# Forgetting attention with mask and maximum in one VectorE operation, fillers at a higher rate, and memory tokens normalised when they are prepared

## Chip, cores and metric

The kernel runs on one core of one Trainium2 chip. The metric is the device time of one execution in microseconds, the median of several runs; lower is better. The engines are TensorE (PE in the profile, with its weight loads as PEld), VectorE (DVE), ScalarE (ACT), GpSimd (POOL) and SyncE (SP), whose queue issues nearly all transfers.

## The reference, cut to what matters

One layer of a hybrid decoder, all float32, 1024 tokens of width 1024, 256 memory tokens:

```python
h = rmsnorm(x, ln1);  z = h @ w_in
ml_out = mlstm(z)                     # 4 heads of width 128
s = q @ k.T * dh**-0.5 + (c_i - c_j)  # forgetting attention, 8 heads of width 64
s = where(qpos >= kpos, s, -inf)
fx_out = softmax(s) @ v
x = x + concat([ml_out, fx_out]) @ w_out
m = rmsnorm(mem, ln_mem)              # memory tokens
x = x + cross_attention(rmsnorm(x, ln_x), m, w_q, w_kv, w_o)
u = relu(rmsnorm(x, ln2) @ w_ff1);  x = x + (u * u) @ w_ff2
out = rmsnorm(x, ln_f)
```

## The kernel before, in words

**Precision and tiles.** Each float32 operand of a projection is split in a high and a low part (`split`, L128 to L136: a copy on ScalarE with rounding, then a subtraction on VectorE), and each product is three matmuls (`mm3`, L182 to L186). Tokens are taken in two halves of 512 columns. SBUF tiles come from pools with few buffers per name (`w2`, names a to y; "f" and "p" have two buffers, "y", "a" one). PSUM has eight banks: sc 3, tp 2, mm, m2 and ov one each. An instruction that wants a buffer waits until its last user is through.

**Order.** Most of the kernel is ordered by a scheduler ahead of the run: each engine gets a fixed list of instructions and works through it in order, and SP has such a list of transfers. So an instruction that waits holds everything behind it on its engine.

**Stages.** The profile's span starts with the loads of x and the first value projection. Then `mem_prepare` (L280 to L294) prepares the memory tokens: for each of four tiles of [128, 2 x 256] it loads the tile into an "f" buffer, adds its squares, multiplies by the gain of ln_mem while splitting (L135 and L136, columns of 256), and stores high and low part to `hmd` in DRAM (L292). At the end it works out the factors 1/rms of the 256 tokens, as columns (`rcol_m`) and as a row over all partitions (`row_m`). The factors are not multiplied in here; they are kept for later. `ml_project` and `ml_head` (L558 to L660, loop L673) then do the four mLSTM heads: projections with a convolution (`conv_silu`, L490 to L510), the carried state of the first half (`carried`, `carry`), and the keys and queries of forgetting attention (`fx_project`, L625 to L636), written to DRAM.

**Forgetting attention** (358 to 587 us of the span). Each of 8 heads has 8 query tiles of 128 rows. `Tile.score` (L715) makes the scores of a query tile in one or two parts of at most 512 columns: two matmuls per part and, in the last part, a third one, of the identity with a triangular constant (L724), which adds -BIG above the diagonal. `Tile.top` (L727) takes the negated maximum of each part on VectorE (L728), and for a second part the minimum of both (L731). `Tile.exp` (L733) is the exponential on ScalarE with that number as bias. `Tile.scale` divides by the sum on GpSimd. `Values` (L749 to L780) transposes the weights (L760), splits them, and multiplies them by the values (L779).

`slot` (L973) issues one step of each of these, in an order written out by hand (`in_order` fixes it on each engine). 13 lead slots issue scores alone; then come 96 value slots (8 heads, 4 + 8 key tiles each), then some that only close.

**Fillers.** Between these steps run independent matmuls, cut into steps with a cost in units: `key_unit` and `value_unit` make the keys and values of cross attention from `hmd` (8 steps of 1.5 for each of 8 + 8 groups), `out_unit` makes the first 5 of 8 slices of the output projection (5 steps of 3.0 for each of 16 groups): 432 units in all. In value slot n, steps are issued until `max(n - DELAY, 0) * RATE` units are spent (L1044: RATE 3.6, DELAY 3), at most to the end of one group. What is left after the slots is issued behind them, in one go (L1053 to L1058). The sink of a key group multiplies by `row_m` (L874) and splits and stores one slot later; that of a value group has `rcol_m` as the scale of its split.

**After it.** `out_proj` (from 607 us) adds the remaining three slices: `mix_load` (L836 to L840) reads what the last heads stored (L794, L795), and `full_sink` loads the partial sum (L1070), adds and stores. Cross attention and the MLP follow; the change doesn't touch them.

Of the kernel before, what the change touches and what calls it, by code (L numbers as in the profile page):

```python
# [9 lines left out]
F32 = mybir.dt.float32  # L10
F32R = mybir.dt.float32r
AF = mybir.ActivationFunctionType
ALU = mybir.AluOpType
# [4 lines left out]
P = 128  # L18
T = 1024
TH = 512  # L20
D = 1024
KT = D // P
NM = 256
# [8 lines left out]
BIG = 1e30  # L32
# [12 lines left out]
def hybrid_layer(ctx: ExitStack, tc: tile.TileContext, a: dict, out: bass.AP):  # L45
    nc = tc.nc
    v, s, g = nc.vector, nc.scalar, nc.gpsimd
# [31 lines left out]
    def w2(tag, n=512, dt=F32, p=P):  # L79
        return sb("r_" + tag, [P, 512], BUFS[tag], dt)[:p, :n]  # L80

    def col(tag, n=1, bufs=3):
        return sb("c_" + tag, [P, 8], bufs)[:, :n]
# [24 lines left out]
    def const(n, shape, dt=F32):  # L108
        return pool.tile(shape, dt, tag=n, name=n, bufs=1)

    load = nc.sync.dma_start
# [4 lines left out]
    ident = const("ident", [P, P])  # L116
    g.memset(ident, 1.0)
    g.affine_select(out=ident, in_=ident, pattern=[[-1, P]], compare_op=ALU.is_equal, fill=0.0, base=0, channel_multiplier=1)
    BF16 = mybir.dt.bfloat16
    identb = const("identb", [P, P], BF16)  # L120
    v.tensor_copy(identb, ident)
    causal = const("causal", [P, P], BF16)
    g.memset(causal, 0.0)
    g.affine_select(out=causal, in_=causal, pattern=[[-1, P]], compare_op=ALU.is_ge, fill=-BIG, base=0, channel_multiplier=1)
    half = const("half", [P, 8])
    g.memset(half, -0.5)
    vec = const("vec", [P, a["vec"].shape[1]])
# [1 line left out]
    def split(hi, lo, src, scale=None):  # L129

        if scale is None:
            s.activation(hi, src, AF.Copy)  # L132
            return v.tensor_tensor(out=lo, in0=src, in1=hi.bitcast(F32), op=ALU.subtract)  # L133
        else:
            s.activation(hi, src, AF.Copy, scale=scale)  # L135
            return v.scalar_tensor_tensor(out=lo, in0=src, scalar=scale, in1=hi.bitcast(F32), op0=ALU.mult, op1=ALU.subtract)  # L136
# [24 lines left out]
    def rotate(*tags):  # L161

        spare[tags] = spare.get(tags, -1) + 1
        return w2(tags[spare[tags] % len(tags)])
# [52 lines left out]
    def square_sum(acc, x, first, by=s, add=v):  # L217
        sq = acc if first else w2("c")[:, : x.shape[-1]]
        if by is s:
            s.activation(sq, x, AF.Square)  # L220
        else:
            by.tensor_tensor(out=sq, in0=x, in1=x, op=ALU.mult)
        if not first:
            add.tensor_tensor(out=acc, in0=sq, in1=acc, op=ALU.add)

    def rsqrt_sums(acc, r, nt, parts=1, bank=None, over=None):

        ps = (bank or ov_)()
        for t in range(nt):
            for e in range(parts):  # L230
                at = (e * nt + t) * P
                nc.tensor.matmul(ps[:, t : t + 1], acc[:, at : at + P], ones, start=e == 0, stop=e == parts - 1)
        rsqrt_cols(r, ps[:, :nt], 1.0 / D, nt, over)
# [10 lines left out]
    def to_row(dst, cols, n, at, bank=None):  # L244

        ps = (bank or ov_)()
        nc.tensor.transpose(ps[:n, :P], cols, ident)
        s.activation(dst[:n, :P], ps[:n, :P], AF.Copy)
        load(at.rearrange("o (t q) -> (o t) q", t=n), dst[:n, :P])
        w = min(dst.shape[1], n * P)  # L250
        return load(dst, at[:, :w].broadcast_to([P, w]))
# [22 lines left out]
    vxd = dram.tile([XH, P, 2, 2, NM], F32, name="vxd")  # L274

    hmd = dram.tile([P, 2, KT, NM], F32, name="hmd")
    row_m = const("row_m", [P, NM])
    rcol_m = const("rcol_m", [P, 2])

    def mem_prepare():  # L280
        acc = w2("b")
        for i in range(KT // 2):
            raw = w2("f")
            load(raw.rearrange("p (k c) -> p k c", k=2), a["mem"][:, 2 * i : 2 * i + 2])
            square_sum(acc, raw, i == 0)
            hi = w2("p", dt=F32R)
            for e in range(2):
                c = slice(e * NM, e * NM + NM)
                gain = vec[:, VEC["ln_mem"] + 2 * i + e :][:, 0:1]
                split(hi[:, c], raw[:, c].bitcast(F32R), raw[:, c], gain)  # L290
            for p_, t in enumerate((hi.bitcast(F32), raw)):
                load(hmd[:, p_, 2 * i : 2 * i + 2], t.rearrange("p (k c) -> p k c", k=2))  # L292
        rsqrt_sums(acc, rcol_m, 2, 2)
        to_row(row_m, rcol_m, 2, rowd[1:2, :NM])  # L294


    xa = act(F32)
# [121 lines left out]
    ps = ov_()  # L419
# [226 lines left out]
    def ml_project(hd):  # L646
        qk = quarters(F32R) if hd % 2 else [w4(dt=F32R) for _ in range(4)]
        q, k = qk[:2], qk[2:]
        yk = conv_silu(MLH + hd, *k)
        next(closing, None)  # L650
        fx_project(0, hd)
        next(closing, None)
        state = carried(hd, yk)
        next(closing, None)
        yq = conv_silu(hd, *q)
        fx_project(1, hd)
        sums = carry(hd, q, yq, *state)
        og = w4()
        for _, hf, ps in proj(weights(a["w_in"][8 + hd]), h, 1):
            o = og[:, hf * TH : hf * TH + TH]  # L660
            v.tensor_tensor(out=o, in0=ps, in1=row[:, hf * TH : hf * TH + TH], op=ALU.mult)
            s.activation(o, o, AF.Tanh, scale=0.5)
        return q, k, og, *sums
# [4 lines left out]
    gate_cols()  # L668
    banks[:] = ["mm", "tp", "m2", "tp"]
    with tc.issue_after(last_sum.ins):  # L670
        mem_prepare()
    ready = ml_project(0)
    for hd in range(MLH):  # L673
        closing = ml_head(hd, *ready)
        next(closing)
        if hd < MLH - 1:
            ready = ml_project(hd + 1)
# [27 lines left out]
    class Tile:  # L705
# [9 lines left out]
        def score(self, e):  # L715
            qs, kh, qs2, kl = (stacks[self.hd % 2][:, i] for i in range(4))
            it = slice(self.i * P, self.wid)
            c0, c1 = self.parts[e]
            c2 = max(c1, c0 + 256)
            sp = sc()  # L720
            nc.tensor.matmul(sp[:, : c2 - c0], qs2[:, it], kl[:, c0:c2], start=True, stop=False)
            nc.tensor.matmul(sp[:, : c2 - c0], qs[:, it], kh[:, c0:c2], start=False, stop=c1 < self.wid)
            if c1 == self.wid:
                nc.tensor.matmul(sp[:, c1 - c0 - P : c1 - c0], identb, causal, start=False, stop=True)  # L724
            self.ps.append(sp[:, : c1 - c0])

        def top(self, e):  # L727
            v.tensor_reduce(out=self.mxs[:, e : e + 1], in_=self.ps[e], axis=mybir.AxisListType.X, op=ALU.max, negate=True)  # L728
            if e:

                v.tensor_tensor(out=self.mxs[:, 1:2], in0=self.mxs[:, 0:1], in1=self.mxs[:, 1:2], op=ALU.min)  # L731

        def exp(self, e):  # L733
            s.activation(self.pt[:, slice(*self.parts[e])], self.ps[e], AF.Exp, bias=self.mxs[:, e : e + 1], accum_out=self.dens[:, e : e + 1])
            if e:
                s.activation(self.mxs[:, 0:1], self.mxs[:, 0:1], AF.Exp, bias=self.mxs[:, 1:2], scale=-1.0)

# [126 lines left out]
    def key_unit(n):  # L864
        def run(ws):
            w = both(ws[0], lambda t: t.rearrange("p (k c) -> p k c", k=KT))
            ps = mm()
            for k in range(KT):
                mm3(ps[:, :NM], both(w, lambda t: t[:, k]), (hm[:, 0, k], hm[:, 1, k]), k == 0, k == KT - 1)
                yield 1.5, k == KT - 1, lambda: sink(ps)  # L870

        def sink(ps):
            t = rotate("p", "a").rearrange("p (e c) -> p e c", e=2)
            v.tensor_tensor(out=t[:, 1], in0=ps[:, :NM], in1=row_m, op=ALU.mult)  # L874

            def store():
                split(t[:, 0].bitcast(F32R), t[:, 1].bitcast(F32R), t[:, 1])
                load(kxd[n // 2, :, :, n % 2], t)

            return store  # L880

        return [a["w_xk"][n]], run

    def value_unit(hd):
        def run(ws):
            ws = [both(w, lambda t: t.rearrange("p (k c) -> p k c", k=4)) for w in ws]
            for t in range(2):
                ps = mm()[:, :NM]
                for k in range(KT):
                    x = (hm[:, 0, k, t * P : (t + 1) * P], hm[:, 1, k, t * P : (t + 1) * P])  # L890
                    mm3(ps, x, both(ws[k // 4], lambda z: z[:, k % 4]), k == 0, k == KT - 1)
                    yield 1.5, k == KT - 1, lambda: sink(t, ps)

        def sink(t, ps):
            o = rotate("p", "a").bitcast(F32R).rearrange("p (e c) -> p e c", e=2)
            split(o[:, 0], o[:, 1], ps, rcol_m[:, t : t + 1])
            load(vxd[hd, :, :, t], o.bitcast(F32))

        return [a["w_xv"][hd, i] for i in range(2)], run
# [141 lines left out]
    banks[:] = ["mm", "m2"]  # L1041
    raw_load()
    raw_load()
    RATE, DELAY = 3.6, 3  # L1044
    n = 0
    while slot(True, max(n - DELAY, 0) * RATE):
        n += 1
# [575 lines left out]
```

## Time and profile before

| | before |
|---|---|
| median of 3 runs | 1543.42 us (1543.1 to 1543.92) |
| the profiled execution | 1541.89 us |
| its span, first to last instruction | 1540.1 us |
| granted TensorE clock | 0.998 |
| VectorE instructions | 1736 |
| ScalarE instructions | 1351 |
| moved by DMA | 303.54 MB, 197 GB/s |

Busy times are shares of the span. In rows of groups the columns are: line, engine, operation, output <- inputs with shapes, count, then busy us and mean ns of one, then the engine's idle time just ahead of them and what ended it. In a timeline the first two numbers are start and length in us. A row with x2 is two instructions that follow each other. Line numbers of a helper (L133, L136, L184 to L186) stand for all its callers; the tiles' names tell them apart: `r_f` is a buffer of name "f", `m`, `mm`, `m2`, `tp`, `sc` and `ov` are PSUM banks.

### The profile page before, as it was taken

To read this page: it belongs to the slowest core of one execution; us is meant where nothing else is said; L and a number is where in the kernel's file an instruction comes from. 1 tells how busy PE (TensorE), PEld (TensorE's weight loads), DVE (VectorE), ACT (ScalarE), POOL (GpSimd) and SP (SyncE) were. 2 spreads that over 40 slices of the span, in tenths; PEclk is the share of its full clock that TensorE was granted. 3 is DMA by queue.
4 is the path that set the end of the run, shared out by engine and by line. 5 is a ranking of instruction groups with operands and counts; after the bars stand their busy time and mean duration, and the time that the engine had idled before them with its cause. 6 is when DMAs were issued, how large, how long until landed. Compare 5 with 4: busy or idle time off the path is not lost. (4 is left out here: it accounts for less than half of the span.)

```text
span 1540.1 us, 22015 instructions
## 1 busy us (share of the span) xinstructions
PE 1508.6 (98%) x7729; PEld 1259.3 (82%) x7729; DVE 1125.5 (73%) x1736; ACT 722.5 (47%) x1351; POOL 480.0 (31%) x515
## 2 busy tenths in 40 slices
PE   8999999999999999999999999999999999999997
PEld 8878888889898887788888877778777688888887
DVE  7656676665788875854457989898897987666666
ACT  7324343334688763543443456666664421111134
POOL 0002130413455441421110024544545543333310
PEclk9999999999999999999999999999999999999999
DMA  6422223436887958953444437766678966666623
GB/s 222 123 79 82 92 101 122 131 125 164 248 259 215 307 173 285 314 186 117 137 142 143 160 132 278 247 254 239 217 256 298 354 259 246 246 246 242 242 90 110
DMA packets 119803, 303.54 MB, mean 197 GB/s; under 512 B 13310, under 2 KB 27960, under 8 KB 111756
## 3 DMA queue, kind: packets, MB, share of 16 engines
q1 hardware_dynamic: 119692, 302.13, 57.4%
q8 instruction: 61, 1.00, 0.3%
q14 instruction: 50, 0.41, 0.1%
HBM read 202.22 MB, written 99.86 MB: 196 GB/s over the span
## 5 line engine op out<-in xcount | busy, mean ns | idle before, releaser
L184 PE MATMUL tp<-act,wl 128*128 128x512 f32 (+1 forms) x448 | 176.4, 394 | 1.5 <-DVE wl L133 0.7
L185 PE MATMUL tp<-act,wh 128*128 128x512 f32 (+1 forms) x448 | 175.3, 391 | 0.0
L186 PE MATMUL tp<-act,wh 128*128 128x512 f32 (+1 forms) x448 | 174.8, 392 | 0.0
L133 DVE TENSOR_TENSOR wl<-wr,wh 128x1024 fp32r<-128x1024 f32 (+2 forms) x99 | 129.5, 1308 | 26.3 <-ACT wh L132 26.0
L132 ACT ACTIVATE wh<-wr 128x1024 fp32r<-128x1024 f32 (+2 forms) x99 | 99.1, 1001 | 85.5 <-PE tp L186 34.7
L184 PE MATMUL mm<-act,wl 128*128 128x512 f32 (+1 forms) x336 | 130.6, 389 | 3.1 <-DVE r_e L1071 1.5
L186 PE MATMUL mm<-act,wh 128*128 128x512 f32 (+1 forms) x336 | 129.0, 384 | 0.0
L185 PE MATMUL mm<-act,wh 128*128 128x512 f32 (+1 forms) x336 | 128.8, 383 | 0.0
L184 PE MATMUL m<-act,wl 128*128 128x512 f32 (+1 forms) x312 | 120.5, 386 | 1.3 <-DVE r_a L916 1.0
L186 PE MATMUL m<-act,wh 128*128 128x512 f32 (+1 forms) x312 | 119.3, 382 | 0.0
L185 PE MATMUL m<-act,wh 128*128 128x512 f32 (+1 forms) x312 | 119.1, 382 | 0.0
L184 PEld LDWEIGHTS tp<-act,wl 128*128 128x128 f32 x448 | 84.2, 188 | 22.2 <-DVE wl L133 2.2
L186 PEld LDWEIGHTS tp<-act,wh 128*128 128x128 f32 x448 | 84.2, 188 | 19.2
L185 PEld LDWEIGHTS tp<-act,wh 128*128 128x128 f32 x448 | 84.2, 188 | 18.7
L184 PE MATMUL sc<-act,wl 128*128 128x512 f32 (+1 forms) x252 | 98.3, 390 | 0.9 <-DVE wl L133 0.8
L1410 POOL TENSOR_TENSOR z<-wr 128x256 f32<-128x256 f32 x56 | 50.7, 925 | 152.0 <-DMA wr<-w_ff2q 139.3
L185 PE MATMUL sc<-act,wh 128*128 128x512 f32 (+1 forms) x252 | 97.8, 388 | 0.0
L186 PE MATMUL sc<-act,wh 128*128 128x512 f32 (+1 forms) x252 | 97.8, 388 | 0.0
L132 ACT ACTIVATE w<-wr 128x768 fp32r<-128x768 f32 (+2 forms) x31 | 25.6, 825 | 146.7 <-PE tp L186 90.7
L132 ACT ACTIVATE wh<-z 128x1024 fp32r<-128x1024 f32 (+1 forms) x54 | 55.4, 1028 | 64.0 <-PE sc L186 26.8
L133 DVE TENSOR_TENSOR wl<-z,wh 128x1024 fp32r<-128x1024 f32 (+1 forms) x54 | 74.9, 1387 | 3.3 <-ACT wh L132 3.1
L184 PEld LDWEIGHTS mm<-act,wl 128*128 128x128 f32 x336 | 63.3, 188 | 16.8 <-DVE r_e L1071 2.0
(676 smaller groups left out, 4252.5 us busy)
## 6 DMA issues: line engine op xcount, KB each, us to landing
act<-right SPq DMA_DIRECT2D x49, 1024.0 KB
right<-w SPq DMA_DIRECT2D x56, 256.0 KB
wr<-w_ff2q SPq DMA_DIRECT2D x28, 512.0 KB
right<-r_d SPq DMA_DIRECT2D x49, 256.0 KB
right<-r_e SPq DMA_DIRECT2D x49, 256.0 KB
act<-fqk SPq DMA_DIRECT2D x48, 256.0 KB
wr<-w_in SPq DMA_DIRECT2D x20, 512.0 KB
wr<-w_ff SPq DMA_DIRECT2D x20, 512.0 KB
```

What stands on the lines that cost most here:

```text
L132: s.activation(hi, src, AF.Copy)
L133: return v.tensor_tensor(out=lo, in0=src, in1=hi.bitcast(F32), op=ALU.subtract)
L184: nc.tensor.matmul(ps, w[1], x[0], start=first, stop=False, skip_group_check=more)
L185: nc.tensor.matmul(ps, w[0], x[1], start=False, stop=False, skip_group_check=more)
L186: nc.tensor.matmul(ps, w[0], x[0], start=False, stop=last, skip_group_check=more)
L1410: g.tensor_tensor(out=o, in0=x, in1=y, op=op)
```

## The change

1. The triangular constant becomes 512 columns wide, with the triangle in its last 128. `score` issues no third matmul. `top` handles the last part of a query tile with one `tensor_tensor_reduce` on VectorE: it adds the constant to the scores, negates, writes the result over the scores in PSUM, and takes the minimum along the row, starting from the first part's number where there is one. The exponential of a last part reads the negated scores, so its scale is -1. First parts keep their reduction. The minimum of two columns goes.
2. `mem_prepare` becomes a generator of two passes. The first loads the four tiles, adds the squares and works out the factors; the row of factors stands in the "y" buffer. The second, called behind `ml_project(0)`, loads the four tiles again, multiplies each by gain and row (two operations of 256 columns), splits it and stores both parts. `row_m` and `rcol_m` no longer exist as constants.
3. The sinks of the key and value groups split straight from PSUM, with no factor; the key sink's store is no longer put off by a slot.
4. RATE is 4.6 instead of 3.6.

```diff
-    causal = const("causal", [P, P], BF16)
+    causal = const("causal", [P, TH], BF16)
...
     def mem_prepare():
         acc = w2("b")
         for i in range(KT // 2):
             raw = w2("f")
             load(pairs_of(raw), a["mem"][:, 2 * i : 2 * i + 2])
             square_sum(acc, raw, i == 0)
+        cols = col("fac", 2)
+        rsqrt_sums(acc, cols, 2, 2)
+        row_m = w2("y")[:, :NM]
+        to_row(row_m, cols, 2, rowd[1:2, :NM])
+        yield
+        for i in range(KT // 2):
+            raw = w2("f")
+            load(pairs_of(raw), a["mem"][:, 2 * i : 2 * i + 2])
             hi = w2("p", dt=F32R)
             for e in range(2):
                 c = slice(e * NM, e * NM + NM)
                 gain = vec[:, VEC["ln_mem"] + 2 * i + e :][:, 0:1]
-                split(hi[:, c], raw[:, c].bitcast(F32R), raw[:, c], gain)
+                v.scalar_tensor_tensor(out=raw[:, c], in0=raw[:, c], scalar=gain, in1=row_m, op0=ALU.mult, op1=ALU.mult)
+            split(hi, raw.bitcast(F32R), raw)
             for p_, t in enumerate((hi.bitcast(F32), raw)):
-                load(hmd[:, p_, 2 * i : 2 * i + 2], t.rearrange("p (k c) -> p k c", k=2))
-        rsqrt_sums(acc, rcol_m, 2, 2)
-        to_row(row_m, rcol_m, 2, rowd[1:2, :NM])
+                load(hmd[:, p_, 2 * i : 2 * i + 2], pairs_of(t))
+        yield
...
     with tc.issue_after(last_sum.ins):
-        mem_prepare()
+        memory = mem_prepare()
+        next(memory)
     ready = ml_project(0)
+    next(memory)
...
-            nc.tensor.matmul(sp[:, : c2 - c0], qs[:, it], kh[:, c0:c2], start=False, stop=c1 < self.wid)
-            if c1 == self.wid:
-                nc.tensor.matmul(sp[:, c1 - c0 - P : c1 - c0], identb, causal, start=False, stop=True)
+            nc.tensor.matmul(sp[:, : c2 - c0], qs[:, it], kh[:, c0:c2], start=False, stop=True)
...
         def top(self, e):
-            v.tensor_reduce(out=self.mxs[:, e : e + 1], in_=self.ps[e], axis=mybir.AxisListType.X, op=ALU.max, negate=True)
-            if e:
-                v.tensor_tensor(out=self.mxs[:, 1:2], in0=self.mxs[:, 0:1], in1=self.mxs[:, 1:2], op=ALU.min)
+            ps = self.ps[e]
+            if e + 1 < len(self.parts):
+                v.tensor_reduce(out=self.mxs[:, e : e + 1], in_=ps, axis=mybir.AxisListType.X, op=ALU.max, negate=True)
+            else:
+                v.tensor_tensor_reduce(
+                    out=ps,
+                    in0=ps,
+                    in1=causal[:, TH - ps.shape[1] :],
+                    scale=-1.0,
+                    scalar=self.mxs[:, 0:1] if e else BIG,
+                    op0=ALU.add,
+                    op1=ALU.min,
+                    accum_out=self.mxs[:, e : e + 1],
+                )
...
-            t = rotate("p", "a").rearrange("p (e c) -> p e c", e=2)
-            v.tensor_tensor(out=t[:, 1], in0=ps[:, :NM], in1=row_m, op=ALU.mult)
-            def store():
-                split(t[:, 0].bitcast(F32R), t[:, 1].bitcast(F32R), t[:, 1])
-                load(kxd[n // 2, :, :, n % 2], t)
-            return store
+            t = rotate("p", "a").bitcast(F32R).rearrange("p (e c) -> p e c", e=2)
+            split(t[:, 0], t[:, 1], ps[:, :NM])
+            load(kxd[n // 2, :, :, n % 2], t.bitcast(F32))
...
-            split(o[:, 0], o[:, 1], ps, rcol_m[:, t : t + 1])
+            split(o[:, 0], o[:, 1], ps)
...
-    RATE, DELAY = 3.6, 3
+    RATE, DELAY = 4.6, 3
```

More of the change, by code (lines that the diff above doesn't have):

```diff
@@ L119, in hybrid_layer @@
     BF16 = mybir.dt.bfloat16
-    identb = const("identb", [P, P], BF16)
-    v.tensor_copy(identb, ident)
-    causal = const("causal", [P, P], BF16)
+    causal = const("causal", [P, TH], BF16)
     g.memset(causal, 0.0)
-    g.affine_select(out=causal, in_=causal, pattern=[[-1, P]], compare_op=ALU.is_ge, fill=-BIG, base=0, channel_multiplier=1)
+    g.affine_select(out=causal, in_=causal, pattern=[[-1, TH]], compare_op=ALU.is_ge, fill=-BIG, base=TH - P, channel_multiplier=1)
     half = const("half", [P, 8])
@@ L276, in hybrid_layer @@
     hmd = dram.tile([P, 2, KT, NM], F32, name="hmd")
-    row_m = const("row_m", [P, NM])
-    rcol_m = const("rcol_m", [P, 2])
     def mem_prepare():
         acc = w2("b")
+        pairs_of = lambda t: t.rearrange("p (k c) -> p k c", k=2)
         for i in range(KT // 2):
             raw = w2("f")
-            load(raw.rearrange("p (k c) -> p k c", k=2), a["mem"][:, 2 * i : 2 * i + 2])
+            load(pairs_of(raw), a["mem"][:, 2 * i : 2 * i + 2])
             square_sum(acc, raw, i == 0)
+        cols = col("fac", 2)
[5 more added lines that the diff above has]
+            raw = w2("f")
+            load(pairs_of(raw), a["mem"][:, 2 * i : 2 * i + 2])
             hi = w2("p", dt=F32R)
@@ L721, in score @@
             nc.tensor.matmul(sp[:, : c2 - c0], qs2[:, it], kl[:, c0:c2], start=True, stop=False)
-            nc.tensor.matmul(sp[:, : c2 - c0], qs[:, it], kh[:, c0:c2], start=False, stop=c1 < self.wid)
-            if c1 == self.wid:
-                nc.tensor.matmul(sp[:, c1 - c0 - P : c1 - c0], identb, causal, start=False, stop=True)
+            nc.tensor.matmul(sp[:, : c2 - c0], qs[:, it], kh[:, c0:c2], start=False, stop=True)
             self.ps.append(sp[:, : c1 - c0])
         def top(self, e):
-            v.tensor_reduce(out=self.mxs[:, e : e + 1], in_=self.ps[e], axis=mybir.AxisListType.X, op=ALU.max, negate=True)
-            if e:
-                v.tensor_tensor(out=self.mxs[:, 1:2], in0=self.mxs[:, 0:1], in1=self.mxs[:, 1:2], op=ALU.min)
+            ps = self.ps[e]
[12 more added lines that the diff above has]
+                )
         def exp(self, e):
-            s.activation(self.pt[:, slice(*self.parts[e])], self.ps[e], AF.Exp, bias=self.mxs[:, e : e + 1], accum_out=self.dens[:, e : e + 1])
+            s.activation(self.pt[:, slice(*self.parts[e])], self.ps[e], AF.Exp, bias=self.mxs[:, e : e + 1], scale=1.0 if e + 1 < len(self.parts) else -1.0, accum_out=self.dens[:, e : e + 1])
             if e:
```

## The prediction

> **What bounds the kernel now.** I read the page's head first: is one engine the limit over the whole span?
>
> ```profile
> span 1540.1 us, 22015 instructions
> PE 1508.6 (98%) x7729; PEld 1259.3 (82%) x7729; DVE 1125.5 (73%) x1736; ACT 722.5 (47%) x1351; POOL 480.0 (31%) x515
> ```
>
> TensorE is busy 98% of the span. So the time is TensorE's issue time plus the few places where it waits, and an edit counts if it takes matmuls out or makes or removes a wait. The profiled execution took 1541.89 us, 1.8 more than its span; the median of the runs is 1543.42, 1.5 above it. I sum against 1541.89 and add the 1.5 at the end.
>
> Next come the busy times by stretch of the attention stage (columns: stretch, its length, busy time and count of PE, PEld, DVE, ACT, POOL, then clock, DMA share, GB/s).
>
> ```profile
> 399.00:440.00 41.00, 39.99 (x290) 35.75 (x289) 33.99 (x83) 34.13 (x92) 20.84 (x31) 1.00 0.74 215
> 440.00:480.00 40.00, 39.97 (x299) 36.54 (x298) 35.23 (x89) 31.06 (x88) 21.53 (x36) 1.00 0.90 270
> 480.00:520.00 40.00, 38.94 (x276) 34.81 (x274) 35.75 (x85) 32.06 (x89) 21.22 (x32) 1.00 0.77 246
> 520.00:560.00 40.00, 40.00 (x230) 32.80 (x229) 32.78 (x82) 29.37 (x83) 18.06 (x32) 1.00 0.80 252
> 560.00:587.00 27.00, 26.87 (x147) 21.96 (x146) 18.48 (x39) 16.41 (x41) 9.35 (x18) 1.00 0.52 174
> 587.00:607.00 20.00, 19.00 (x82) 14.88 (x81) 7.66 (x11) 4.81 (x10) 3.51 (x4) 1.00 0.89 303
> ```
>
> The granted clock is 1.00 throughout. Even here TensorE stays the limit; VectorE comes closest, 35.75 of 40 us (89%) in the third stretch, where TensorE loses 1.1 us. From 587 to 607 the leftover fillers run without attention, and VectorE is nearly free.
>
> Last, the table of TensorE's waits, for 20 to 130 us and then for 380 to 600 us.
>
> ```profile
> PE m L184 <- DVE act L136: 1.3, 1, 1.3
> PE mm L184 <- DVE r_c L518: 0.9, 1, 0.9
> ```
>
> ```profile
> PE m L184 <- DVE r_a L916: 1.0, 1, 1.0
> PE ov L779 <- DVE r_f L789: 0.9, 2, 0.7
> ```
>
> There is little waiting to win: 2.2 us early, about 2 in attention.
>
> **Mask matmuls gone.** The timeline of TensorE shows the price of one:
>
> ```profile
> 381.20 0.28 PE L721 MATMUL sc<-act 128*128 128x256 f32 x1
> 381.32 0.28 PE L722 MATMUL sc<-act 128*128 128x256 f32 x1
> 381.44 0.23 PE L724 MATMUL sc<-causal,identb 128*128 128x128 bf16 x1
> 381.48 0.36 PE L184 MATMUL m<-wh,act 128*128 128x256 f32 x1
> 381.68 0.28 PE L185 MATMUL m<-wl,act 128*128 128x256 f32 x1
> ```
>
> Matmuls overlap, so starts count, not lengths. From L722 to the second matmul behind the mask are 0.36 us; the neighbours of this shape start 0.12 apart, so two steps would take 0.235. The mask costs 0.125 to 0.13, I take 0.128.
>
> ```profile
> L724 PE MATMUL sc<-causal,identb x64: 229/229/233, 358.4 to 564.5; 128*128 128x128 bf16 x64
> ```
>
> 64 x 0.128 = **-8.2 us**. The Trainium skill, "TensorE: Matmul & The Clock Gate", section Back-to-back issue gap, gives about 81 ns per matmul of 128 columns in a sustained stream; by it the sum would have 5.2 us here. The rows above, in which the mask stands between matmuls of another type, speak for the larger one.
>
> **The fused VectorE operation.** Groups by form, 399 to 600 us on VectorE, then one on ScalarE (whole span):
>
> ```profile
> L728 DVE TENSOR_REDUCE c_mx<-sc 128x1 f32<-128x512 f32 x42 | 28.6, 680 | 0.2
> L133 DVE TENSOR_TENSOR r_e<-tp,r_d 128x512 fp32r<-128x512 f32 x32 | 21.9, 684 | 6.5 <-ACT r_d L132 6.3
> L728 DVE TENSOR_REDUCE c_mx<-sc 128x1 f32<-128x384 f32 x14 | 7.7, 548 | 0.1
> L731 DVE TENSOR_TENSOR c_mx<-c_mx 128x1 f32<-128x1 f32 x28 | 7.1, 253 | 1.0
> L728 DVE TENSOR_REDUCE c_mx<-sc 128x1 f32<-128x256 f32 x14 | 5.8, 411 | 0.0
> L728 DVE TENSOR_REDUCE c_mx<-sc 128x1 f32<-128x128 f32 x13 | 3.6, 276 | 0.0
> L874 DVE TENSOR_TENSOR r_p<-mm,row_m 128x256 f32<-128x256 f32 x4 | 1.6, 408 | 0.0
> L874 DVE TENSOR_TENSOR r_a<-m,row_m 128x256 f32<-128x256 f32 x4 | 1.6, 406 | 0.0
> ```
>
> ```profile
> L734 ACT ACTIVATION_READ_ACCUMULATOR act<-sc,c_mx 128x1 f32 x64 | 12.9, 202 | 0.0
> ```
>
> A subtraction with a second operand and an SBUF output (684 ns) costs what the reduction costs (680): the second operand is free. No row of before shows VectorE writing PSUM, or this instruction, so its body is unknown. Lower bound: the reduction's price. Upper: a pass for each of its two operations, twice that; the 64 last parts are 16 of each width, mean (680+548+411+276)/4 = 479 ns, so +30.7 us. I take the lower one, since reading a second operand and writing a full tile are both free in the 684 ns row. In the built program each of these operations is two VectorE instructions, the second of one column. The Trainium skill, "VectorE: DVE Perf Modes", section Two Vector instructions with no wait between them, says so too: an operation that writes out its accumulator is a main instruction and an accumulator read; no run yet shows VectorE's price for it. The nearest row is ScalarE's read, 202 ns: 0 to 0.2 each, upper value 64 x 0.202 = +12.9. Off go L731 (32 x 0.25 = 7.8) and L874 (8 x 0.407 = 3.3). VectorE in 399 to 607: 163.9 of 208 us now (79%); then 163.9 + 12.9 - 11.1 = 165.7 of some 201 (82%). Beside TensorE's work that is hidden: **0**, with the cover gone only if the body doubles (rival 2).
>
> **Rate.** The eight heads make 96 value slots, fed some 335 of 432 units of fillers (93 x 3.6); the rest runs densely in 587 to 607. With 4.6 (93 x 4.6 = 428) all is spent inside the slots. TensorE's work is the same; each slot carries more of it for the same softmax, so VectorE's peaks go down. I take **-1** (0 to -2, the two waits of the table: L789's 0.9, and the 1.1 of 480 to 520 which partly is the same). The L916 wait belongs to the dense tail and goes too, **-1.2**. Against it: output projection now follows right behind the last slot and needs the last head's rows.
>
> ```profile
> 580.42 0.32 SPq L795 DMA_DIRECT2D mix<-r_f  x1
> 580.91 0.34 SPq L934 DMA_DIRECT2D wr<-w_out_a  x1
> 581.29 0.46 SPq L908 DMA_DIRECT2D r_a<-x  x1
> 581.79 1.43 SPq L839 DMA_DIRECT2D act<-mix  x2
> ...
> 585.96 0.40 PE L779 MATMUL ov<-w,w 128*128 128x256 f32 x2
> ```
>
> Here the store at 580.42 is 5.6 us ahead of the last value matmul, some 6 to 7 ahead of the slot's end. Behind it: store 2.4 (below), and two loads of 768 KB at 303 GB/s (last stretch), 5.2: 7.6, with a load of x queued between up to 10. It lands 1 to 3 late in the worst order; filler of the last slots covers some: **+1.8** (0 to 3). Net tail +0.6.
>
> **Memory tokens.** Pass 1 has only the squares, and no split and store that hold the buffers, so the early wait on L136 goes (ScalarE stood 2.24 us for a reload there, the 44.05 row), and the L518 one probably: **-2** (0 to -2.2). Pass 2 lies between 130 and 170 us: four reloads that are new, 8 gain multiplications, 4 subtractions of 512 columns, 8 stores. In the built program all four tiles use the same one of two buffers, since the other holds the head's carried sum: each reload waits for the store of the tile before.
>
> ```profile
> 37.58 1.72 SPq L292 DMA_DIRECT2D hmd<-r_f  x2
> 40.02 0.33 SPq L284 DMA_DIRECT2D r_f<-mem  x1
> ```
>
> ```profile
> 44.05 0.63 ACT L220 ACTIVATE r_c<-r_f 128x512 f32<-128x512 f32 x1 [2.24 <-DMA r_f<-mem]
> ```
>
> That is such a round trip in before: store issued 37.58, reload 40.02 (2.44), data used 44.05 (4.03): 6.5. It ran beside a 512 KB weight load; for a quieter place I estimate 5.0. Where the trips stand in VectorE's order is read from the built program against these rows of before:
>
> ```profile
> 135.59 0.95 DVE L133 TENSOR_TENSOR r_e<-r_c,r_d 128x256 fp32r<-128x256 f32 x2 [0.60 <-ACT r_d L132]
> ...
> 145.00 1.21 DVE L133 TENSOR_TENSOR wl<-wr,wh 128x1024 fp32r<-128x1024 f32 x1
> ...
> 151.16 0.68 DVE L631 SCALAR_TENSOR_TENSOR r_p<-tp,row 128x512 f32<-128x512 f32 x1
> ...
> 154.43 1.21 DVE L503 SCALAR_TENSOR_TENSOR z<-z,z 128x1024 f32<-128x1024 f32 x1
> ```
>
> ```profile
> 155.08 0.39 PE L184 MATMUL mm<-act,wl 128*128 128x512 f32 x1
> ```
>
> The first tile's subtraction stands between the two of the 135.59 row, done at 137.2. The second tile arrives at 142.2 (trip 5.0) or 143.7 (6.5); its subtraction stands behind the weight split of 145.00, done at 146.9 or 148.4. The third arrives at 151.9 or 154.9, its subtraction stands behind L503: 156.0 or 157.7. The fourth arrives at 161 or 164.2. And L631, which empties a bank of PSUM at 151.16 now, stands behind the fourth tile's multiplications: 0.9 + 0.7 later, 162.5 or 165.7. TensorE's first matmul of the next projection, at about 155.1, waits for that bank, and all its queue with it. Wait 7 to 11: **+9** (0 if the order of the queues decides less than I think).
>
> **Sum**: -8.2 + 0 - 1 + 0.6 - 2 + 9 = -1.6; 1540.3 against 1541.89, so 1541.8 on the median's scale.
>
> **Rivals.** (1) *Pass 2 hidden*: round trips are short, or the fourth tile is through before TensorE needs the bank. Speaks for it: DMA share is low there. Against: three trips would have to shrink below 3 us each. Time: -8.2 - 2 - 1 + 0.6 = -10.6, 1532.8. (2) *VectorE becomes the bound* (slower): the fused operation in place in PSUM takes two passes or more. At twice, VectorE has 165.7 + 30.7 = 196 of 201 us (98%): from there on it decides. At 2.5 times it has 212, +11: 1552.8. For it: no row shows such an operation. Against: the 684 ns row. (3) *Trips are loaded* like those of 37.58 or more: wait 14, 1546.8. (4) *The masks were hidden work*: TensorE then waits for softmax instead, -8.2 becomes 0: 1550; against it, the stretches with PE at 39.97 of 40. By the gap of the Trainium skill ("TensorE: Matmul & The Clock Gate", Back-to-back issue gap) the forecast would be 3.0 us higher, 1544.8, inside its own range.
>
> **Chances.** About 0.2% (3.1 us) is what a measurement here can tell from no change. Forecast 0.55 (own range 1538 to 1546: 0.20 of it below 1540.3, 0.31 within, 0.04 above), rival 1 0.20 (faster), rivals 2 and 4 0.18 (slower), rival 3 0.07 (0.03 within, 0.04 slower). Faster 0.40, same 0.34, slower 0.26. The range, 1532 to 1551, leaves out the ends of rivals 1 and 2.
>
> **What would show it.** Right: no L724; a TensorE wait of 7 to 11 us between 150 and 170, released by VectorE's r_p, with VectorE idle on a reload from mem; the 45 us wait gone; VectorE under 90% from 400 to 600. Wrong: no wait at 155 (rival 1); fused rows far above 0.7 us at 512 columns and TensorE waiting for them (rival 2); a wait above 3 us ahead of the output projection.

## The result, and the profile after

| | before | after |
|---|---|---|
| median | 1543.49 us (4 runs, 1543.1 to 1543.92) | 1558.53 us (4 runs, 1556.88 to 1560.21) |
| ratio after / before | | 1.0104 (95% interval 1.0092 to 1.0116) |
| the profiled execution | 1541.89 us | 1556.88 us |
| its span | 1540.1 us | 1554.8 us |
| ahead of the first score matmul | 358.2 us | 372.3 us |
| from there to the end | 1181.9 us | 1182.5 us |

The change costs 15 us where 1.6 were forecast as a gain. The head of the page after:

```profile
span 1554.8 us, 21923 instructions
PE 1506.9 (97%) x7665; PEld 1258.9 (81%) x7665; DVE 1120.2 (72%) x1763; ACT 719.5 (46%) x1347; POOL 479.1 (31%) x515
```

TensorE has 64 matmuls fewer and is busy 1.7 us less, yet the span is 14.7 longer: the loss is waiting, and work at a lower clock behind the waits. (The profiled execution after is the fastest of its four, 1.7 us below their median.) Where it lies is told by one landmark, the first score matmul. Its group in the profile of each kernel, before and then after (where the same line is L728), gives the first and the last start:

```profile
L721 PE MATMUL sc<-act x96: 276/391/497, 358.2 to 564.1; 128*128 128x512 f32 x48, 128*128 128x256 f32 x32, 128*128 128x384 f32 x16
```

```profile
L728 PE MATMUL sc<-act x96: 277/390/501, 372.3 to 599.1; 128*128 128x512 f32 x48, 128*128 128x256 f32 x32, 128*128 128x384 f32 x16
```

14.1 us are lost ahead of forgetting attention, in the mLSTM heads, where the memory tokens are prepared. From there to the end the kernel is not faster either, although 64 x 0.128 = 8.2 us of matmuls are gone there. So there are two questions. (The last score comes later, 599.1, mainly because the fillers now run between the scores.)

The first one is answered by TensorE's waits after, 130 to 300 us (columns: wait, total, times, longest):

```profile
PE tp L182 <- DVE r_p L636: 7.0, 1, 7.0
PE tp L521 <- DVE z L508: 4.0, 1, 4.0
PE sc L213 <- ACT r_c L595: 1.5, 1, 1.5
PE m L182 <- DVE c_m L543: 0.3, 1, 0.3
```

and VectorE's timeline after, in the same place:

```profile
135.29 0.42 DVE L131 TENSOR_TENSOR r_e<-r_c,r_d 128x256 fp32r<-128x256 f32 x1
140.56 0.88 DVE L295 SCALAR_TENSOR_TENSOR r_f<-r_f,vec,r_y 128x256 f32<-128x256 f32 x2 [4.85 <-DMA r_f<-mem]
...
152.83 0.88 DVE L295 SCALAR_TENSOR_TENSOR r_f<-r_f,vec,r_y 128x256 f32<-128x256 f32 x2 [4.37 <-DMA r_f<-mem]
153.62 1.22 DVE L508 SCALAR_TENSOR_TENSOR z<-z,z 128x1024 f32<-128x1024 f32 x1
...
161.52 0.88 DVE L295 SCALAR_TENSOR_TENSOR r_f<-r_f,vec,r_y 128x256 f32<-128x256 f32 x2 [3.19 <-DMA r_f<-mem]
162.32 0.68 DVE L636 SCALAR_TENSOR_TENSOR r_p<-tp,row 128x512 f32<-128x512 f32 x1
```

Three of the four memory tiles arrive one after the other (L295 at 140.6, 152.8, 161.5), VectorE is idle in front of each, and L636, which TensorE needs, stands behind the last. L508, for which TensorE waits 4.0 us, stands behind the third in the same way. The waits of SP's queue, 130 to 165 us, show why the tiles come one by one: each of the three reloads (L290) was held until the store of the tile before had landed.

```profile
SPq L290 <- DMA hmd<-r_f: 8.0, 3, 4.7
```

Then the granted clock falls (windows; the value behind POOL's is the clock):

```profile
150.00:163.00 13.00, 2.02 (x8) 1.09 (x6) 6.46 (x9) 3.15 (x4) 0.10 (x1) 0.62 0.37 121
163.00:167.00 4.00, 3.94 (x10) 3.13 (x11) 1.38 (x2) 1.42 (x4) 0.00 (x0) 0.52 0.34 131
167.00:170.00 3.00, 3.00 (x15) 2.42 (x14) 1.50 (x4) 1.88 (x4) 0.52 (x2) 1.00 0.45 175
```

TensorE is at work again at 163 but at 0.52 until 167: 4 x 0.48 = 1.9 us more. 11.0 + 1.9 + 1.8 (the two later waits) - 2.2 (the early waits on L136 and L518, which are gone: the table for 0 to 130 us has only the wait at the very start that before has too) = 12.5 of the 14.1; the remaining 1.6 us were not traced.

For the second question, the waits after from 380 to 600 us, against 1.9 for the two main rows of before:

```profile
PE sc L728 <- ACT w L750: 5.4, 3, 3.9
PE sc L728 <- ACT act L750: 1.7, 3, 0.7
PE ov L795 <- DVE r_f L805: 1.7, 4, 1.0
PE tp L776 <- DVE r_b L134: 0.8, 1, 0.8
```

A score waits for the exponential (L750) that frees its PSUM bank. ScalarE's timeline after shows what held the longest of them:

```profile
475.03 0.63 ACT L957 ACTIVATE wh<-wr 128x512 fp32r<-128x512 f32 x1 [5.41 <-DMA wr<-w_xv]
475.56 0.26 ACT L130 ACTIVATE r_d<-tp 128x128 fp32r<-128x128 f32 x1
475.72 0.57 ACT L750 ACTIVATE w<-sc,c_mx 128x384 f32<-128x384 f32 x1
```

ScalarE stood 5.41 us for a filler's weights, with the exponential queued behind. SP's timeline shows that transfer's issue, among those of the next head's queries, keys and decay:

```profile
464.32 0.61 SPq L710 DMA_DIRECT2D act<-fqk  x1
465.04 0.53 SPq L945 DMA_DIRECT2D wr<-w_xv  x1
466.46 0.44 SPq L710 DMA_DIRECT2D act<-fqk  x1
467.71 1.16 SPq L710 DMA_DIRECT2D act<-decay  x2
```

512 KB issued at 465.04 and used at 475.03: 10.0 us. ScalarE began to wait for it 4.6 us behind the issue. The fused operation itself is cheap (groups by form, 399 to 640 us):

```profile
L735 DVE TENSOR_REDUCE c_mx<-sc 128x1 f32<-128x512 f32 x31 | 21.1, 681 | 0.1
L738 DVE DVE_READ_ACCUMULATOR2_ANT c_mx<- 128x1 f32 x59 | 8.1, 137 | 0.1
L738 DVE CUSTOM_DVE_ANT_0 sc<-sc,causal,c_mx 128x512 f32<-128x512 f32 x8 | 6.0, 755 | 0.4
L738 DVE CUSTOM_DVE_ANT_0 sc<-sc,causal 128x512 f32<-128x512 f32 x7 | 4.8, 681 | 0.0
```

681 ns for 512 columns like the reduction, 755 with the first part's number, and 137 for the read. That is 0.14 to 0.21 us beyond a reduction, and L731 (0.25) is gone where a query tile has two parts. VectorE's busy time between 480 and 520 us falls from 35.75 to 28.99 us of 40, and no stretch of 40 us between 400 and 640 has more than 31.82.

### The profile page after: what moved, and what is told of

Read it like the earlier page. It is cut to its first block, busy times and chain, and to the rows that moved or that the text cites. A ratio compares the mean times of both kernels' runs of the same rounds, so it can differ in the third digit from the quotient of the medians.

```text
span 1554.8 us, 21923 instructions
## 1 busy us (share of the span) xinstructions
PE 1506.9 (97%) x7665; PEld 1258.9 (81%) x7665; DVE 1120.2 (72%) x1763; ACT 719.5 (46%) x1347; POOL 479.1 (31%) x515
## 5 line engine op out<-in xcount | busy, mean ns | idle before, releaser
L183 PEld LDWEIGHTS mm<-act,wh 128*128 128x128 f32 x336 | 63.2, 188 | 13.9 <-ACT r_c L218 1.6
```

The lines of the kernel that those rows point to most:

```text
L183: nc.tensor.matmul(ps, w[0], x[1], start=False, stop=False, skip_group_check=more)
```

## The experiments

The theory: pass 2 goes through one buffer in series, and the waiting transfer holds VectorE; and the attention stage waits for transfers that the masks' time and the lower rate covered. The rival: the fused operation slows the softmax chain. Beside each time stands the median of the kernel before in the same group of runs; "ahead" and "rest" are the span up to and from the first score matmul (before 358.2 and 1181.9). These two come from the one profiled execution of each kernel, and executions of one kernel lie 2 to 8 us apart (1535.8 to 1543.6 for the kernel that keeps its tiles), so a difference of 1 to 3 us between two rests shows nothing by itself; what a part is worth is read from the medians.

**The parts alone.** The fused operation alone; to make room for the wide constant beside `row_m`, most small column buffers have one buffer instead of three:

```diff
-    def col(tag, n=1, bufs=3):
+    def col(tag, n=1, bufs=None):
+        bufs = bufs or (3 if tag in ("mx", "den", "rden") else 1)
```

> The kernel before with the fused mask and maximum alone: old preparation of the memory tokens, old sinks, rate 3.6. To make room for the wide constant, eight names of small column buffers have one buffer instead of three. Theory (the loss of the change lies in pass 2 and in the rate; the fused operation only wins its 64 matmuls): 1543.5 - 8.2 = 1535, with the waits of the attention stage as before (some 5 us). Rival (the fused operation brings the new waits of the attention stage, +9.8 us of lost TensorE time there): 1543.5 - 8.2 + 9.8 = 1545.

Measured 1540.47 against 1542.74, ratio 0.9987 (0.9978 to 0.9997). Ahead 359.8, rest 1180.7. Neither end: the fused operation helps, by some 2 us and not 8.

The memory part alone (`mem_prepare`, its two calls and the sinks of the changed kernel):

> The kernel before with the two-pass preparation of the memory tokens and the sinks without factor alone. Theory: pass 2 stops TensorE for 11 us between 150 and 165 us, and with what follows it costs 13.7 there and 3.8 up to 300 us, while 3.0 are won before 100 us: 1543.5 + 14.5 = 1558. Rival (only the wait of 11 us counts, the remainder belongs to another part): 1543.5 + 11 - 3 = 1551.5.

1562.95 against 1542.74, 1.0136 (1.0121 to 1.0151): +20, more than the whole change, and 5 above the theory. Ahead 376.3: all but 2 of it lies ahead of attention. The waits around 155 us are there (4.6 and 6.7), and here the clock is down behind the later wait of 1.5 us at 248 us too, 0.62 over 9 us, where in the profile after it stays at 1.00:

```profile
248.00:257.00 9.00, 7.47 (x24) 6.11 (x24) 3.76 (x14) 1.38 (x3) 1.66 (x1) 0.62 0.00 0
```

The rate alone:

```diff
-    RATE, DELAY = 3.6, 3
+    RATE, DELAY = 4.6, 3
```

> The kernel before with RATE 4.6 alone. Theory (a higher rate asks for the weights of the fillers sooner than the transfers bring them, ScalarE stands for them ahead of an exponential, and TensorE waits for that exponential): +7 to +10 in the attention stage, -1.2 at its tail: 1549 to 1552. Rival (the attention waits come from the fused operation): 1541 to 1543.5.

1549.66, 1.0048 (1.0033 to 1.0063): +7. Ahead 358.7, rest 1189.6. ScalarE's timeline and TensorE's waits (396 to 630 us) of this kernel, which has no fused operation:

```profile
461.49 0.63 ACT L946 ACTIVATE wh<-wr 128x512 fp32r<-128x512 f32 x1 [5.14 <-DMA wr<-w_xv]
```

```profile
PE sc L721 <- ACT w L734: 5.8, 4, 3.7
PE tp L184 <- DMA act<-mix: 2.0, 1, 2.0
```

The wait of the changed kernel is here without the fused operation, so the rival falls; and the wait for `mix` ahead of the output projection, forecast as 1.8, is 2.0. The three parts alone add up to about 25 us (-2, +20 and +7) where the whole change costs 15, so none of them is worth its lone figure inside the change.

The changed kernel with RATE 3.6:

> The changed kernel with RATE 3.6. Theory: the waits of the attention stage fall back to some 5 us and the tail's come back, 1558.5 - 9.8 + 1.2 = 1550. Rival (they come from the fused operation): 1558.5 to 1560.

1558.84, 1.0111 (1.0094 to 1.0128), the same as after: the number is the rival's, and the theory's 1550 is missed. The rival's cause does not hold all the same: TensorE's waits for the exponential (L750) fall from 7.1 us in all to 1.3 with the fused operation in place. Ahead 377.3, rest 1179.0. In the two profiles the rest is 3.5 lower at the old rate, where the theory had 8.6, and 5.0 are lost ahead, most of it to the low clock again, behind the wait at 248 us as in the kernel with the memory part alone. The rate only acts later, so the loss ahead does not come from it. One profile of each can't tell what the rate is worth here; the runs with the tiles kept, below, can.

**The chain through one buffer.** One of the seven large tiles (`act`) is free while pass 2 runs, so its reloads can go in parallel:

```diff
         yield
+        whole = act(F32).rearrange("p a b -> p (a b)")
         for i in range(KT // 2):
-            raw = w2("f")
+            raw = whole[:, i * 512 : i * 512 + 512]
             load(pairs_of(raw), a["mem"][:, 2 * i : 2 * i + 2])
```

> The changed kernel, but the second pass takes its four reloads into one free large tile of 16 KB per partition instead of one after the other into the single free buffer f. Place, instructions and bytes are the same. Theory (the cost is the chain of store, reload and multiplication through one buffer): the wait of 11 us between 150 and 165 us and the low clock behind it are gone, 1558.5 - 14 to -17 = 1541 to 1545. Rival (the second pass costs by being there, through VectorE's queue and the transfers): 1555 or more.

1545.14 against 1542.59, 1.0008 (0.9994 to 1.0023). Ahead 358.7 instead of 372.3: 13 of the 15 us are gone. But the place did not stay the same. With a free tile to load into, the four reloads are issued at 69.6 us instead of one by one from 115.7 to 157.5, and the eight multiplications run together at 86.6, where they stood between 126 and 162:

```profile
86.58 3.25 DVE L296 SCALAR_TENSOR_TENSOR act<-act,vec,r_y 128x256 f32<-128x256 f32 x8 [1.99 <-DMA r_y<-rowd]
```

A wait of 2.3 us is new at this early place (on L524). The rival falls: the second pass doesn't cost by being there. What costs is the single buffer, by the chain and by the late place that goes with it; no run here prices the two apart.

The four tiles kept in the large tile from pass 1 on, no reload, and RATE 3.6:

```diff
+        whole = act(F32).rearrange("p a b -> p (a b)")
         for i in range(KT // 2):
-            raw = w2("f")
+            raw = whole[:, i * 512 : i * 512 + 512]
             load(pairs_of(raw), a["mem"][:, 2 * i : 2 * i + 2])
...
         yield
         for i in range(KT // 2):
-            raw = w2("f")
-            load(pairs_of(raw), a["mem"][:, 2 * i : 2 * i + 2])
+            raw = whole[:, i * 512 : i * 512 + 512]
```

> The changed kernel without reloads at all: the four tiles stay in the free large tile from pass 1 to pass 2; and RATE 3.6. Theory (the chain is the cost of the memory part, 3.6 the better rate): early waits gone (-3), masks gone with some of it given back as in the run with the fused operation alone (-2 to -3), no chain: 1542.7 - 5 to -6 = 1537 to 1538. Rival (the sinks or the row in the y buffer cost too): 1542 or more.

1538.54, 0.9981 (0.9969 to 0.9994): faster than both kernels, if by only 4 us against the kernel before. Here too the multiplications stand early, at 97 us. Ahead 356.8, rest 1182.3.

Both passes ahead of the first projection, RATE 3.6:

```diff
         next(memory)
+        next(memory)
     ready = ml_project(0)
-    next(memory)
```

> The changed kernel with RATE 3.6 and the second pass asked for right behind the first, ahead of the first projection, where both buffers f are free. Theory: the chain runs through two buffers and ahead of the carried state, so the wait at 150 to 165 us is gone: 1538 to 1543. Rival (the scheduler's order for a second pass always underrates the round trip, wherever it stands): a wait of some us between 50 and 110 us, 1546 or more.

1543.56, 1.0008 (0.9997 to 1.0019). Ahead 361.2, so the rival has a part: waits of 1.7 us on L508 and 1.1 on L523 stand at the earlier place, and 3 us are lost against the old order. Against the run that keeps its tiles, 1538.54, reloads through two buffers at the early place cost 5 us.

**What eats the masks' 8 us.** A lower rate, fused operation alone:

> The fused mask and maximum alone, as in the first run, with RATE 3.2. Theory (without the masks the slots are shorter, while the weights of the fillers still come at their own pace, so that ScalarE waits for them; a lower rate per slot gives them time): the waits for w_xv go, but more fillers are left for the tail: 1538 to 1540.5. Rival (the waits come from VectorE's chain in the slot): as the first run or slower, 1540.5 to 1543.

1547.26, 1.0030 (1.0017 to 1.0043). Rest 1185.4. This theory fell, and the time lies outside both ranges: ScalarE still waits for w_xv, 4.23 us here against 2.85 in the first run. The rate moves weights and head loads against each other; slower isn't safer. Where the whole 7 us against the first run lie was not traced.

Tiles kept, RATE 4.6:

> The changed kernel (RATE 4.6) with the four tiles kept from pass 1 to pass 2, no reloads. Theory (without the chain the rate costs what it cost alone in the kernel before, +7): 1538.5 + 5 to 7 = 1543.5 to 1545.5, as the run with the wide reload. Rival (in the changed kernel the rate is neutral, as 1558.5 against 1558.8 suggested): 1538.5.

1541.77 against 1542.12, 0.9991 (0.9981 to 1.0001), rest 1185.4. The time lies between theory and rival: against 3.6 the higher rate costs 3 us. That the rate looked neutral in the changed kernel fits its larger loss ahead at 3.6 (377.3 against 372.3), but with one profile of each this is not shown.

Tiles kept, mask matmuls as before, RATE 3.6:

> The kernel before (mask matmuls, RATE 3.6) with the new sinks and the two-pass preparation that keeps its tiles. Theory (the fused operation is worth some 2.5 us, the rest of its 8 goes into waits for transfers; the memory part without the chain wins the 3 of the early waits): 1542.6 - 2 to -3 = 1540 to 1540.5. Rival (the fused operation wins its whole 8): 1546.

1540.59, 0.9989 (0.9980 to 0.9998), 2.1 above the run with the fused operation (1.2 by the ratios): worth 1 to 2 us again, and here without the edit of the column buffers.

Tiles kept, RATE 4.6, without the head loads:

```diff
-            if hd + 2 < FXH:
-                fx_load(hd + 2)
```

> As the run with tiles kept and RATE 4.6, but the loads of queries, keys and decay for heads 2 to 7 (8 transfers a head, 1.5 MB) are left out, so heads 2 to 7 work on the data of heads 0 and 1. Theory (those bursts delay the filler's weights, ScalarE stands for w_xv and w_xk, TensorE behind it): the waits at 460 and 490 go, 5 to 8 less: 1537 to 1539. Rival (the rate costs through VectorE's and ScalarE's own work in the slot): 1543 to 1545, unchanged.

1529.18, 0.9913 (0.9898 to 0.9928): 12.6 below the same kernel with the loads, about twice what was expected. Rest 1172.9. ScalarE's waits for transfers from 399 to 600 us, with the loads and then without:

```profile
ACT wh L957 <- DMA wr<-w_xv: 8.1, 2, 5.2
ACT wh L957 <- DMA wr<-w_out_a: 5.1, 4, 2.4
ACT wh L957 <- DMA wr<-w_xk: 2.2, 1, 2.2
```

```profile
ACT wh L955 <- DMA wr<-w_xk: 0.8, 1, 0.8
```

Without the loads the weights w_xk, 512 KB like w_xv, land 3.5 us behind their issue. The stretches 440 to 520 us with the loads and without:

```profile
440.00:480.00 40.00, 36.27 (x261) 34.45 (x260) 28.65 (x76) 26.33 (x74) 19.03 (x28) 0.96 0.75 223
480.00:520.00 40.00, 37.57 (x238) 33.69 (x237) 28.08 (x80) 27.77 (x78) 20.03 (x31) 0.96 0.90 263
```

```profile
440.00:480.00 40.00, 39.97 (x301) 38.07 (x299) 32.00 (x88) 31.20 (x86) 22.88 (x32) 1.00 0.60 197
480.00:520.00 40.00, 39.95 (x247) 34.97 (x246) 33.22 (x86) 29.84 (x84) 19.04 (x32) 1.00 0.85 286
```

TensorE is busy 39.95 of 40 us with VectorE and ScalarE doing more, not less: their work was not the limit here. The same with RATE 3.6:

> As the run with tiles kept and RATE 3.6, with the same loads left out. Theory: it had 4 us of lost time at 460 to 480 us from the same wait, so 1538.5 - 3 to -4 = 1535, and the difference between the two rates falls below 3. Rival: 1538.5, unchanged.

1534.20, 0.9948 (0.9933 to 0.9962), rest 1176.2. The weights w_xv land 4.2 us behind their issue here (median). Without these transfers the higher rate wins 5 us; with them it loses 3. And the kernel before without them:

> The kernel before with the loads of queries, keys and decay for heads 2 to 7 left out (these heads work on the data of heads 0 and 1). It tells what the transfers cost the kernel before, so what the fused operation is worth without them: the run with tiles kept, RATE 3.6 and no head loads took 8 less than the kernel before. Theory (the transfers' waits eat most of the masks' 8 us in the changed one, few in the one before): 1540 to 1542. Rival (the head loads cost both the same 4 us): 1538.

1541.83 against 1542.50, 0.9996 (0.9987 to 1.0005), rest 1184.5. The loads cost the kernel before nothing that can be measured. From this run to the one ahead of it are 7.6 us, of which the memory part without its chain has 1.5 to 2, if it wins without the head loads what it won with them: the fused operation is worth about 6 where the head loads don't interfere, and 2 where they do. TensorE's busy time agrees, for this run and then for the one ahead of it:

```profile
PE 1509.1 (98%) x7729; PEld 1259.6 (82%) x7729; DVE 1126.7 (73%) x1736; ACT 722.3 (47%) x1351; POOL 482.2 (31%) x515
PE 1500.6 (98%) x7665; PEld 1258.8 (82%) x7665; DVE 1120.8 (73%) x1763; ACT 720.4 (47%) x1347; POOL 485.8 (32%) x515
```

64 matmuls fewer are 8.5 us less, 0.133 each. With the head loads in place the fused operation alone takes only 4.7 us off TensorE's busy time (1508.6 to 1503.9), and TensorE's idle time, span less busy, grows by 5.1.

**Spreading the head loads**, tiles kept, RATE 4.6 and 3.6:

```diff
-            fx_step()
+            tick[0] += 1
+            if tick[0] % 3:
+                fx_step()
+            elif tick[0] == 9:
+                fx_step()
+                fx_step()
```

> Tiles kept, RATE 4.6, all loads in place, but the eight transfers of a head are spread over eleven slots instead of eight (one in two of three slots, both decay transfers in the ninth). Theory (the burst delays the filler's weights): 1534 to 1539. Rival (the volume, not the burst, is what counts, or the later head loads are late for their scores): 1541 to 1545.

1540.91 against 1542.50, 0.9987 (0.9975 to 0.9998).

> The same spreading with RATE 3.6. Theory: the wait of some 4 us at 460 to 480 us shrinks: 1535 to 1537.5. Rival: 1538.5 or more, as with the loads in one run.

1538.31, 0.9979 (0.9968 to 0.9990), as without the spreading. They don't tell a burst from the volume, since the edit spread the loads over the slots but not over time: SP's timeline of the faster rate shows the eight transfers going out from 445.3 to 452.6 us. Without the spreading they went out from 445.9 to 452.1, in the same order. In both, SP's queue had been held ahead of them until a store to `mix` landed, 2.6 us with the spreading.

```profile
445.34 1.13 SPq L712 DMA_DIRECT2D act<-fqk  x2
446.56 0.55 SPq L910 DMA_DIRECT2D vxd<-r_p  x1
447.17 2.10 SPq L712 DMA_DIRECT2D act<-fqk  x3
449.38 0.52 SPq L947 DMA_DIRECT2D wr<-w_xv  x1
450.55 0.44 SPq L712 DMA_DIRECT2D act<-fqk  x1
```

What stays open: burst or volume, and what a real schedule of these transfers could win of the 12.6 us.

## Why the prediction was wrong, point by point

**Pass 2 (+9): mechanism right, size too small.** The places and times hold closely: the second tile was forecast at 142 to 144 and is used at 140.6, the third at 152 to 155 (152.8), the fourth at 161 to 164 (161.5), L636 behind it at 162.5 to 166 done (163.0), TensorE's wait for that bank 7 to 11 (7.0). Part of this agreement is luck: from the end of one tile's split to the use of the next were 5.2, 8.2 and 6.1 us, where the forecast took 5.0 to 6.5 for each, and the chain began 1.8 us earlier than forecast (135.4 against 137.2). The term lacked three things: a second wait, 4.0 us, since the convolution's L508 stands behind the third tile's multiplications; 1.9 us at half clock behind the long wait; and 1.8 us of later waits at 195 and 248 us, the latter with the clock down again in two other runs. In place of +9 the profile shows 16.3: 14.1, and the 2.2 of early waits that were won. Taking the reloads out of the single buffer wins back 13 us (the wide reload), leaving them out 17 (tiles kept, RATE 4.6).

**Masks (-8.2), and the cover: this step failed.** The sum took TensorE to be the only limit from 358 us on, since it is busy 39.97 of 40 us, and booked every matmul as time. The price of a mask matmul was right: 0.133 us where 0.128 was taken. With the head loads left out the term is nearly right (about 6). With them it is 2: the prediction asked whether VectorE could keep up, and it can; it didn't ask whether the filler's weights could. Their transfer took 10.0 us from issue to use in the changed kernel, beside the head loads, and ScalarE waits for it, in order, ahead of the exponentials.

**Rate (-1, and +0.6 at the tail): failed with it.** VectorE's peaks did go down, as said, but this was not the limit. Alone the rate costs 7, with the tiles kept 3. The wait for `mix` in the tail was right (2.0 where the rate acts alone).

**The fused operation (0): right.** 681 ns like the reduction and 137 for the read, within the bounds; the rival in which VectorE becomes the bound falls. Rival 4, in which the masks were hidden work, is in part what happened, through transfers and not through softmax.

**Early waits (-2): right.** Both are gone, and the runs with tiles kept, ahead 355.2 to 356.8, show 1.4 to 3.0.

Sum of the profile: 14.1 ahead (forecast 9 - 2) and 0.6 from there (forecast -8.6). All the signs that the prediction named for being right did come: no L724, a wait of 7 us behind a reload from `mem`, the early wait gone, VectorE under 90%. None of them looked at ScalarE's waits for weights. And the rivals were priced one at a time: rivals 3 and 4 together, 5 and 8.2 above the forecast, would have given 1555.

## What to carry to other kernels

A reload through a single free buffer is a chain of store, reload and use; count its round trips, and look at who stands behind the waiting instruction in the engine's order. When matmuls are taken out of a stage in which TensorE is at 99%, ask of every transfer in it how long before its use it is issued: here the time taken out was also the transfers' time. A rate that was tuned against one set of transfers says nothing for another; here the same step from 3.6 to 4.6 costs 3 to 7 us with the head loads (in the changed kernel nothing that can be measured) and wins 5 without.

## What the runs showed of the hardware

A wait of TensorE can cost more than its length. Behind the waits of 4.0 and 7.0 us, which only four short matmuls part, the granted clock is 0.52 for 4 us of full work; behind one of 1.5 us it fell to 0.62 over 9 us in one run and stayed at 1.00 in another. The Trainium skill, "TensorE: Matmul & The Clock Gate", Part 1, describes this gate: half clock after idleness, full clock after about 3.4 us of sustained work. The 4 us behind the two waits agree; that the low clock can stand behind a wait of only 1.5 us, the rows for 248 to 257 us show.

A VectorE operation that reads and writes PSUM in place with a second operand costs 681 ns at 512 columns, the same as a plain reduction (755 where it starts from a column in SBUF), and its accumulator read 137 ns, less than ScalarE's 202.
